# Expert weights loaded in 8 KB runs, projection steps of two k-tiles by 1024 columns, and moving tiles placed 32 bytes from the stationary ones

## The chip, the core and the metric

The kernel runs on one core of a Trainium2 chip. The metric is device time in microseconds of one execution. The matmul engine is TensorE (PE, with its weight loads as PEld), the elementwise engines are VectorE (DVE), ScalarE (ACT) and GpSimd (POOL); SyncE (SP) issues nearly all loads, in one queue.

## What is computed

Two transformer blocks of two layers each, on 256 tokens of width 1024, all in float32. Every layer starts from an adaptive projection of a condition vector to six vectors of 1024 (shift, scale and gate for two halves of the layer). The first block has two attentions and a feed-forward part with a short convolution; the second block has a mixer over tokens and a context, and 16 experts of which each takes the 32 tokens that score highest for it. In the first layer of the second block tokens and context go through the experts (two groups), in the last layer the tokens alone.

```python
mod = silu_c @ w_ada[l] + b_ada[l]                # 1024 -> 6 * 1024
sh1, sc1, gt1, sh2, sc2, gt2 = split(mod, 6)
h = modulate(rmsnorm(x, g_mix[l]), sh1, sc1)
x = x + gt1 * latent_mixer(h @ w_in[l], ...)
h2 = modulate(rmsnorm(x, g_ffn[l]), sh2, sc2)
...
def expert_choice_ffn(h, w_router, w_g, w_u, w_d):
    gate, idx = lax.top_k(softmax(h @ w_router), 32)     # tokens of each expert
    xs = h[idx]
    y = (silu(xs @ w_g) * (xs @ w_u)) @ w_d              # 1024 x 1024 each, 16 experts
    return zeros_like(h).at[idx].add(y * gate)
```

## The kernel before

Activations lie with channels on partitions, in eight k-tiles of 128 channels by 256 tokens. The dense matmuls work in split form: `split` (L226 to L228) writes a weight as a rounded high part `wh` (ACT, L227) and the rest `wl` (DVE, L228), activations likewise (`hh`, `hl`; in attention and feed-forward also in tiles `k1`, `k8`, `pt`), and `mm3` (L239 to L246) issues three products at L245: high by high, high by low, low by high. The stationary operand is the weight, the moving one the 256 tokens. In the trace's names buffer numbers are left out, so `k1`, `k8`, `k4` and `k2` all read `k`: into `dd`, `k` is a `k8` tile; into `acc`, a `k1` tile.

Tiles that matmuls read lie in pools, one behind the other (`PLACES`, L42): first the weights and their loads, then `hh`, `hl`, `k1`, `k8`, `pt`. Ahead of each pool stands a gap of `PADS` float32 words (L43). All tiles are multiples of 256 bytes, so the sum of the gaps so far gives a tile's place mod 256 against the weights (at 0): `hh` 64, `hl` 96, `k1` 128, `k8` 0, `pt` 32.

The adaptive projection is `ada` (L384 to L458). Part of its output, `DIRECT` (L37) blocks of 1024 columns, is made by `chunk`: one load of all eight k-tiles by 256 columns (in DRAM, runs of 1 KB), eight fp32 matmuls into four column tiles of one PSUM tile (L404), a DVE copy (L407), two PE transposes (L410), a reduction (L414) and the bias (L394). The other blocks are summed on DVE (L435 to L448) from loads of 4 KB runs. Eight chunks run at startup for the first layer, 24 for each layer of the second block as fillers between other work, from 476 to 1124 us; in the first block's second layer there are none.

The expert weights, three matrices of 1024 x 1024 for each of 16 experts, come as 192 loads of 1 MB a layer, in groups of four experts, issued by `expert_loads` (L1196 to L1231) through SP in the order of use; a load waits until its tile is free. A load holds two k-tiles, rows `(2 kp + k) P + p`, so that each of 128 partitions gets two runs of 4 KB. Loads with the tags `k4` and `whl` go to two tiles (`HALVES`, L40), each with a load of its own. In the last group the third matrix comes in columns of 256 instead, with runs of 1 KB. `product` (L1237) issues the fp32 matmuls at L1249: for each pair of k-tiles, each group of tokens, two k-tiles, two halves of 512 columns and four experts that share the array as column tiles. Its result is transposed at L1274 (eight transposes for each group of tokens and of experts), multiplied with the third matrix, and scattered back (L1282, L1283). The tokens are gathered ahead of it (L1161 to L1182) by a matmul with a one-hot matrix, whose stationary operand is 128 channels of the tokens (L1176 to L1180). The order of the instructions on PE between these parts is written by the tile planner when the program is built.

Of the kernel before, what the change touches and what calls it, by code (L numbers as in the profile page):

```python
# [13 lines left out]
OP = mybir.AluOpType  # L14
AX = mybir.AxisListType
PSUM = bass.MemoryType.PSUM

P = 128
S = 256
D = 1024  # L20
KT = D // P
# [4 lines left out]
N_EXP = 16  # L26
CAP = 32
GE = 4
# [11 lines left out]
HALVES = {"k4": ("k4", "k4"), "whl": ("wh", "wl")}  # L40
BUFS = {"k4": N4, "wh": NH, "wl": 3}
PLACES = [("wh", "wl", "w", "k2", "k4", "rx", "rr"), ("hh",), ("hl",), ("k1",), ("k8",), ("pt",)]  # L42
PADS = [0, 16, 8, 8, 32, 8]  # L43
PAD = 32

CONST_WIDTHS = [
# [79 lines left out]
class Kernel:  # L126
# [256 lines left out]

    def ada(self, w, cc, cs, bias, ns, direct):  # L384
        mod = self.t([P, ns, 48], "mod", 2)
        state = {}

        def bias_add(ps, c0, nj):
            for s in range(ns):
                i = bias[0][:, c0:c0 + nj]  # L390
                o = mod[:, s, c0:c0 + nj]
                if len(ps[s].shape) == 3:
                    o, i = (a.rearrange("p (g j) -> p j g", j=4) for a in (o, i))
                self.nc.vector.tensor_tensor(o, ps[s], i, op=OP.add)  # L394

        def chunk(c):
            def go():
                nc = self.nc
                t = self.wload(w, 0, KT, 256 * c, 256, tag=self.ada_tags.pop(0) if self.ada_tags else self.ada_tag)
                ad = self.ad()[:, :256]  # L400
                for i in range(2):
                    for g in range(4):
                        k = 2 * g + i
                        nc.tensor.matmul(ad[32 * g:32 * g + 32], cs[:, k], t[:, k], start=i == 0, stop=i == 1,  # L404
                                         skip_group_check=True)
                r = self.k1([P, 256])
                nc.vector.tensor_copy(r, ad)  # L407
                ps = self.mm((P, 2, P))
                for j in range(2):
                    nc.tensor.transpose(ps[:, j], r[:, j * P:(j + 1) * P], self.c("ident"))  # L410
                q = self.tiny([P, ns, 2])
                m = 32 // ns
                for s in range(ns):
                    nc.vector.tensor_reduce(q[:, s], ps[:, :, m * s:P:32], axis=AX.X, op=OP.add)  # L414
                bias_add([q[:, s] for s in range(ns)], 2 * c, 2)
            return go

        def total(b):
# [28 lines left out]
                            nc.vector.scalar_tensor_tensor(a, t[:, j], f, a, op0=OP.mult, op1=OP.add)  # L447
            return go  # L448

        todo = [chunk(c) for c in ([0, 4, 1, 5, 2, 6, 3, 7] if ns == 1 else range(8))[:4 * direct]]  # L450
        todo += [chunk(c) for c in range(8, 4 * direct)]
        for b in range(direct, 6):
            todo += [summed(b, c) for c in range(4)]
            if ns == 2 or b == 5:
# [698 lines left out]
    def again(self, x, a, b, r, put):  # L1153
        for k in range(KT):
# [3 lines left out]
            put(k, h)  # L1158
            yield

    def gather(self, s, th, tl, xs):  # L1161
        nc = self.nc
        e = slice(32 * s, 32 * s + N_EXP)
        ps = self.mm((P, 2, N_EXP))
        for t in range(2):
            nc.tensor.transpose(ps[:, t], self.sa[e, t * P:(t + 1) * P], self.c("ident")[e, e])
        st = self.k1([P, 2, N_EXP])
        nc.vector.tensor_copy(st, ps)
        hot = [self.k2([P, N_EXP, CAP], F32R) for _ in range(2)]
        for t in range(2):  # L1170
            nc.vector.tensor_tensor(hot[t], self.c("iota")[:, None, :].to_broadcast([P, N_EXP, CAP]),
                                    st[:, t, :, None].to_broadcast([P, N_EXP, CAP]), op=OP.is_equal)
        yield
        for k in range(KT):
            ps = self.mm()
            a = slice(k * P, (k + 1) * P)  # L1176
            for t in range(2):
                b = hot[t].rearrange("p e c -> p (e c)")
                nc.tensor.matmul(ps, th[:, t, a], b, start=t == 0, stop=False)
                nc.tensor.matmul(ps, tl[:, t, a], b, start=False, stop=t == 1)  # L1180
            nc.scalar.copy(xs[k // 4][:, k % 4], ps)
            yield  # L1182
# [13 lines left out]
    def expert_loads(self, l, early, ring):  # L1196
        ws = [self.io[n][l] for n in ("w_e_gate_2", "w_e_up_2", "w_e_down_2")]
        todo = [(ws[which][GE * gi + e], kp, which == 2 and gi == N_EXP // GE - 1) for gi in range(N_EXP // GE)
                for which in range(3) for kp in range(4) for e in range(GE)]
# [2 lines left out]

        def load(t, w, kp, cols, k, n):
            if cols:
                src = w[P * k:P * (k + n), 256 * kp:256 * kp + 256]
            else:
                src = w[(2 * kp + k) * P:(2 * kp + k + n) * P]
            self.nc.sync.dma_start(t, src.rearrange("(k p) n -> p k n", p=P))  # L1208

        def more(n):  # L1210
            late = []
# [21 lines left out]
    def experts(self, l, groups, gather, done):  # L1233
        nc, io = self.nc, self.io
# [20 lines left out]
        for gi in range(N_EXP // GE):  # L1255
# [11 lines left out]
            for s in range(ns):  # L1267
                tt = self.wl([P, KT, P], F32)
                for n in range(2):
                    a = acts[s][:, 512 * n:512 * n + 512]  # L1270
                    nc.vector.tensor_tensor(a, a, pu[s][n], op=OP.mult)  # L1271
                    ps = self.dd((P, 4, P))
                    for i in range(4):
                        nc.tensor.transpose(ps[:, i], a[:, i * P:(i + 1) * P], self.c("ident"))  # L1274
                    nc.scalar.copy(tt[:, 4 * n:4 * n + 4], ps)
                actt.append(tt)
            down = lambda s, k, e: actt[s][:, k, 32 * e:32 * e + 32]
# [208 lines left out]
```

## Time and profile before

| | us |
|---|---|
| median of the runs shown | 2833.57 |
| lowest and highest of them | 2826.25, 2837.12 |
| the profiled execution | 2828.94 |
| its span | 2827.2 |
| PE busy | 2637.7 (93%) |
| DVE busy | 1406.4 (50%) |
| ACT busy | 1023.5 (36%) |
| DMA, mean rate | 263 GB/s of 742.61 MB |

The span covers the first to the last instruction of the profiled execution; the remaining 1.7 us lie around it. The page of the profile shows shares over the whole span; what holds in one stage is read from the slices and from tables by stretches. In a row of instructions the first name is the tile that is written, behind the arrow stand the tiles that are read.

### The profile page before, as it was taken

How to read it: one execution, taken by the hardware profiler on the slowest of the kernel's cores; microseconds unless marked ns; L12 is line 12 of the kernel's file. 1: busy time of each engine (PE TensorE's matmuls, PEld its weight loads, DVE VectorE, ACT ScalarE, POOL GpSimd, SP SyncE). 2: the span in 40 equal slices, each digit the busy share in tenths (PEclk: the TensorE clock that was granted, in tenths of full speed). 3: DMA queues.
4: the chain of work that ended last, by engine and by line, in shares of the span. 5: the costliest groups of instructions: out<-in, count | busy, mean ns of one | idle time of the engine just before them, and what ended most of it. 6: DMA issues, size and time to landing. Idle time of an engine off the chain costs nothing.

```text
span 2827.2 us, 45431 instructions
## 1 busy us (share of the span) xinstructions
PE 2637.7 (93%) x18816; PEld 1835.7 (65%) x18816; DVE 1406.4 (50%) x2791; ACT 1023.5 (36%) x1906; POOL 123.2 (4%) x139
## 2 busy tenths in 40 slices
PE   7998999999999999989999999999989998878876
PEld 5898998888998689856994333333556994212122
DVE  6989977766778755776552010010577562000001
ACT  3564555554555644445453100000455452000000
POOL 0100001000000000120011000000021001000000
PEclk9999999999999999989999999999999999999999
DMA  8788855586455478412655999999712775999999
GB/s 310 242 314 290 309 176 169 186 277 240 163 193 191 151 257 266 138 43 80 204 164 221 366 401 404 420 388 409 248 60 75 250 235 222 420 420 420 421 420 344
DMA packets 397692, 742.61 MB, mean 263 GB/s; under 512 B 16214, under 2 KB 270126, under 8 KB 397486
## 3 DMA queue, kind: packets, MB, share of 16 engines
q1 hardware_dynamic: 396398, 738.66, 71.5%
q8 instruction: 148, 2.42, 0.3%
q10 hardware_dynamic: 1088, 1.05, 0.1%
q14 instruction: 58, 0.48, 0.0%
HBM read 738.61 MB, written 1.05 MB: 262 GB/s over the span
## 4 chain that ended last, share of the span: by engine, by line
PE 39%; DMA 12%; DVE 3%; POOL 1%; SPq 1%; ACT 1%; issue 0%; DVEq 0%; POOLq 0%; ACTq 0%
PE dd L245 12%; PE acc L1249 12%; PE mm L1249 5%; DMA w<-in_w_e_up_dram 2%; DMA k<-in_w_e_down_dram 2%; PE acc L941 2%; DMA w<-in_w_e_down_dram 2%; DMA k<-in_w_e_gate_dram 2%; DMA k<-in_w_e_up_dram 2%; DMA w<-in_w_e_gate_dram 2%; PE mm L970 1%; PE mm L964 1%; PE acc L1301 1%; PE dd L1282 1%; POOL k L756 1%; SPq L1208 1%
## 5 line engine op out<-in xcount | busy, mean ns | idle before, releaser
L245 PE MATMUL dd<-hh,wh 128*128 128x256 f32 x2384 | 684.4, 288 | 17.6 <-ACT hh L269 13.9
L228 DVE TENSOR_TENSOR wl<-w,wh 128x1024 fp32r<-128x1024 f32 (+1 forms) x534 | 554.5, 1042 | 276.7 <-ACT wh L227 275.2
L245 PE MATMUL dd<-hh,wl 128*128 128x256 f32 x2384 | 677.9, 285 | 5.6 <-DVE wl L228 5.6
L245 PE MATMUL dd<-hl,wh 128*128 128x256 f32 x2384 | 678.9, 285 | 0.7 <-DVE hl L481 0.5
L227 ACT CAST wh<-w 128x1024 fp32r<-128x1024 f32 (+1 forms) x534 | 477.9, 900 | 554.4 <-PE dd L245 424.4
L245 PEld LDWEIGHTS dd<-hh,wh 128*128 128x128 f32 x2384 | 454.2, 191 | 42.9 <-ACT hh L269 15.6
L245 PEld LDWEIGHTS dd<-hh,wl 128*128 128x128 f32 x2384 | 451.7, 190 | 12.5 <-DVE wl L228 6.9
L245 PEld LDWEIGHTS dd<-hl,wh 128*128 128x128 f32 x2384 | 452.6, 190 | 10.2 <-issue 7.2
L1249 PE MATMUL acc<-w,pt 128*32 128x512 f32 x624 | 222.9, 597 | 31.7 <-DMA w<-in_w_e_up_dram 17.0
L1271 DVE TENSOR_TENSOR wh<-wh,acc 128x512 f32<-128x512 f32 x20 | 13.7, 687 | 451.2 <-PE acc L1249 451.2
L1249 PE MATMUL acc<-k,pt 128*32 128x512 f32 x692 | 224.9, 597 | 8.7 <-DMA k<-in_w_e_up_dram 5.1
L245 PE MATMUL dd<-k,wh 128*128 128x256 f32 x896 | 168.6, 287 | 0.8 <-DVE k L655 0.5
L756 POOL TENSOR_TENSOR k<-k,rope 32x256 f32<-32x256 f32 (+1 forms) x96 | 86.8, 904 | 1820.7 <-DVE k L900 1332.4
L1249 PE MATMUL acc<-w,k 128*32 128x512 f32 x480 | 160.3, 603 | 0.7 <-ACT pt L1149 0.7
L1249 PE MATMUL acc<-w,wl 128*32 128x512 f32 x396 | 139.8, 600 | 15.9 <-DMA w<-in_w_e_down_dram 15.9
L1249 PE MATMUL acc<-k,wl 128*32 128x512 f32 x432 | 146.6, 600 | 5.1 <-DMA k<-in_w_e_down_dram 5.1
L245 PEld LDWEIGHTS dd<-k,wh 128*128 128x128 f32 x896 | 140.7, 192 | 4.5 <-DVE k L655 1.4
L1249 PE MATMUL acc<-k,k 128*32 128x512 f32 x376 | 133.4, 605 | 0.0
L1249 PEld LDWEIGHTS acc<-w,pt 128*32 128x32 f32 x624 | 45.8, 109 | 133.7 <-issue 69.9
L245 PE MATMUL dd<-k,wl 128*128 128x256 f32 x448 | 127.5, 285 | 2.1 <-DVE wl L228 2.1
L1283 DVE SCALAR_TENSOR_TENSOR x_res<-dd,mod,x_res 128x256 f32<-128x256 f32 x64 | 28.9, 483 | 173.0 <-PE dd L1282 173.0
L941 PE MATMUL acc<-k,k 64*128 64x512 f32 (+1 forms) x192 | 94.5, 606 | 14.8 <-ACT k L269 9.5
(351 smaller groups left out, 4408.5 us busy)
## 6 DMA issues: line engine op xcount, KB each, us to landing
w<-in_w_in_dram SPq DMA_DIRECT2D x104, 1024.0 KB
w<-in_w_ada_dram SPq DMA_DIRECT2D x63, 1024.0 KB
w<-in_w_e_gate_dram SPq DMA_DIRECT2D x54, 1024.0 KB
w<-in_w_e_up_dram SPq DMA_DIRECT2D x54, 1024.0 KB
w<-in_w_e_down_dram SPq DMA_DIRECT2D x48, 1024.0 KB
w<-in_w_up_dram SPq DMA_DIRECT2D x44, 1024.0 KB
k<-in_w_e_gate_dram SPq DMA_DIRECT2D x43, 1024.0 KB
k<-in_w_e_down_dram SPq DMA_DIRECT2D x43, 1024.0 KB
```

Source lines behind the costliest of these rows:

```text
L227: self.nc.scalar.copy(h, src)
L228: self.nc.vector.tensor_tensor(l, src, h.bitcast(F32), op=OP.subtract)
L245: self.last_mm = self.nc.tensor.matmul(ps, a, b, start=first and i == 0, stop=last and i == len(ops) - 1, skip_group_check=group)
L756: nc.gpsimd.tensor_tensor(u[dst], q[src], sin[src], op=OP.mult)
L941: nc.tensor.matmul(ps[:, :n], q[a, mt, qb * P:(qb + 1) * P], kk[a, br, lo:512], start=True, stop=not mask, skip_group_check=True)
L964: nc.tensor.transpose(pp[:, i], e[:, i * P:(i + 1) * P], self.c("ident"))
L970: nc.tensor.matmul(po[64 * f:64 * f + 64], vv[:, kt, P * br + 64 * f:P * br + 64 * f + 64], pt[:, f, i], start=i == 0, stop=i == len(kts) ...
L1208: self.nc.sync.dma_start(t, src.rearrange("(k p) n -> p k n", p=P))
L1249: nc.tensor.matmul(accs[s][n][32 * e:32 * e + 32], lhs(s, 2 * kp + k, e), tiles[e][k][:, 512 * n:512 * n + 512], start=kp == 0 and k == 0, ...
L1282: nc.tensor.matmul(ps, y[:, k * P:(k + 1) * P], maps[s][:, gi], start=True, stop=True)
L1283: nc.vector.scalar_tensor_tensor(x[:, k], ps, gate[:, k:k + 1], x[:, k], op0=OP.mult, op1=OP.add)
L1301: nc.tensor.matmul(ps[32 * e:32 * e + 32], down(s, k, e), tiles[e][k], start=k == 0, stop=k == KT - 1, skip_group_check=True)
```

## The change

Three things change. `PADS` moves the gaps: the places mod 256 become `hh` 32, `hl` 32, `k1` 160, `k8` 32, `pt` 32. The direct part of the projection goes in steps of two k-tiles by 1024 columns (runs of 4 KB): eight matmuls a step as before, four steps to a block of 1024 columns. With one condition vector (at startup) the four steps add up in one PSUM tile; with two, DVE copies the first and adds the others into a tile `adr`. Copy (or the last addition), two transposes and the bias follow only the fourth step; the reduction is gone. The expert loads, except the last group's columns, take rows `2 p + k` instead: a tile of two k-tiles gets one run of 8 KB on each partition, a half one of 4 KB at every 8 KB. Which channels a k-tile holds changes with it, so the stationary operands of the gather and of the transposes (first three groups) take every second column (`paired`).

```diff
--- before.py
+++ after.py
@@ -40,7 +40,7 @@
 HALVES = {"k4": ("k4", "k4"), "whl": ("wh", "wl")}
 BUFS = {"k4": N4, "wh": NH, "wl": 3}
 PLACES = [("wh", "wl", "w", "k2", "k4", "rx", "rr"), ("hh",), ("hl",), ("k1",), ("k8",), ("pt",)]
-PADS = [0, 16, 8, 8, 32, 8]
+PADS = [0, 8, 0, 32, 32, 0]
 PAD = 32
 
 CONST_WIDTHS = [
@@ -383,36 +383,47 @@
 
     def ada(self, w, cc, cs, bias, ns, direct):
         mod = self.t([P, ns, 48], "mod", 2)
-        state = {}
+        state, hold = {}, ns == 1
 
         def bias_add(ps, c0, nj):
             for s in range(ns):
                 i = bias[0][:, c0:c0 + nj]
                 o = mod[:, s, c0:c0 + nj]
                 if len(ps[s].shape) == 3:
-                    o, i = (a.rearrange("p (g j) -> p j g", j=4) for a in (o, i))
+                    o, i = (a.rearrange("p (g j) -> p j g", j=ps[s].shape[1]) for a in (o, i))
                 self.nc.vector.tensor_tensor(o, ps[s], i, op=OP.add)
 
-        def chunk(c):
+        def direct_step(b, c):
             def go():
                 nc = self.nc
-                t = self.wload(w, 0, KT, 256 * c, 256, tag=self.ada_tags.pop(0) if self.ada_tags else self.ada_tag)
-                ad = self.ad()[:, :256]
-                for i in range(2):
+                t = self.wload(w, 2 * c, 2, 1024 * b, 1024, tag=self.ada_tags.pop(0) if self.ada_tags else self.ada_tag)
+                if hold:
+                    ad = state[b] = self.acc((P, 256)) if c == 0 else state[b]
+                else:
+                    ad = self.ad()[:, :256]
+                for j in range(2):
                     for g in range(4):
-                        k = 2 * g + i
-                        nc.tensor.matmul(ad[32 * g:32 * g + 32], cs[:, k], t[:, k], start=i == 0, stop=i == 1,
+                        nc.tensor.matmul(ad[32 * g:32 * g + 32], cs[:, 2 * c + j], t[:, j, 256 * g:256 * g + 256],
+                                         start=j == 0 and (c == 0 or not hold), stop=j == 1 and (c == 3 or not hold),
                                          skip_group_check=True)
-                r = self.k1([P, 256])
-                nc.vector.tensor_copy(r, ad)
+                if hold:
+                    if c < 3:
+                        return
+                    r = self.k1([P, 256])
+                    nc.vector.tensor_copy(r, ad)
+                elif c == 0:
+                    r = state[b] = self.t([P, 256], "adr", 1)
+                    nc.vector.tensor_copy(r, ad)
+                else:
+                    r = state[b]
+                    nc.vector.tensor_tensor(r, r, ad, op=OP.add)
+                if c < 3:
+                    return
                 ps = self.mm((P, 2, P))
                 for j in range(2):
                     nc.tensor.transpose(ps[:, j], r[:, j * P:(j + 1) * P], self.c("ident"))
-                q = self.tiny([P, ns, 2])
                 m = 32 // ns
-                for s in range(ns):
-                    nc.vector.tensor_reduce(q[:, s], ps[:, :, m * s:P:32], axis=AX.X, op=OP.add)
-                bias_add([q[:, s] for s in range(ns)], 2 * c, 2)
+                bias_add([ps[:, :, m * s:P:32] for s in range(ns)], 8 * b, 8)
             return go
 
         def total(b):
@@ -447,8 +458,7 @@
                             nc.vector.scalar_tensor_tensor(a, t[:, j], f, a, op0=OP.mult, op1=OP.add)
             return go
 
-        todo = [chunk(c) for c in ([0, 4, 1, 5, 2, 6, 3, 7] if ns == 1 else range(8))[:4 * direct]]
-        todo += [chunk(c) for c in range(8, 4 * direct)]
+        todo = [direct_step(b, c) for b in range(direct) for c in range(4)]
         for b in range(direct, 6):
             todo += [summed(b, c) for c in range(4)]
             if ns == 2 or b == 5:
@@ -1158,6 +1168,9 @@
             put(k, h)
             yield
 
+    def paired(self, k):
+        return slice(256 * (k // 2) + k % 2, 256 * (k // 2) + 256, 2)
+
     def gather(self, s, th, tl, xs):
         nc = self.nc
         e = slice(32 * s, 32 * s + N_EXP)
@@ -1173,7 +1186,7 @@
         yield
         for k in range(KT):
             ps = self.mm()
-            a = slice(k * P, (k + 1) * P)
+            a = self.paired(k)
             for t in range(2):
                 b = hot[t].rearrange("p e c -> p (e c)")
                 nc.tensor.matmul(ps, th[:, t, a], b, start=t == 0, stop=False)
@@ -1202,10 +1215,10 @@
 
         def load(t, w, kp, cols, k, n):
             if cols:
-                src = w[P * k:P * (k + n), 256 * kp:256 * kp + 256]
+                src = w[P * k:P * (k + n), 256 * kp:256 * kp + 256].rearrange("(k p) n -> p k n", p=P)
             else:
-                src = w[(2 * kp + k) * P:(2 * kp + k + n) * P]
-            self.nc.sync.dma_start(t, src.rearrange("(k p) n -> p k n", p=P))
+                src = w[2 * kp * P:(2 * kp + 2) * P].rearrange("(p k) n -> p k n", k=2)[:, k:k + n]
+            self.nc.sync.dma_start(t, src)
 
         def more(n):
             late = []
@@ -1271,7 +1284,8 @@
                     nc.vector.tensor_tensor(a, a, pu[s][n], op=OP.mult)
                     ps = self.dd((P, 4, P))
                     for i in range(4):
-                        nc.tensor.transpose(ps[:, i], a[:, i * P:(i + 1) * P], self.c("ident"))
+                        b = slice(i * P, (i + 1) * P) if gi == N_EXP // GE - 1 else self.paired(i)
+                        nc.tensor.transpose(ps[:, i], a[:, b], self.c("ident"))
                     nc.scalar.copy(tt[:, 4 * n:4 * n + 4], ps)
                 actt.append(tt)
             down = lambda s, k, e: actt[s][:, k, 32 * e:32 * e + 32]
```

## Rows read from the trace of the kernel before

**Rows 1.** Page, span in 40 slices: PE's busy tenths, and the transfer rate.
```profile
PE   7998999999999999989999999999989998878876
...
GB/s 310 242 314 290 309 176 169 186 277 240 163 193 191 151 257 266 138 43 80 204 164 221 366 401 404 420 388 409 248 60 75 250 235 222 420 420 420 421 420 344
```

**Rows 2.** Table by stretches: busy us (count) PE, PEld, DVE, ACT, POOL; clock, DMA, GB/s.
```profile
11.00:28.00 17.00, 13.71 (x119) 8.00 (x123) 9.31 (x30) 5.47 (x13) 0.00 (x0) 1.00 1.09 385
100.00:350.00 250.00, 239.87 (x1884) 227.37 (x1884) 234.48 (x362) 135.90 (x225) 0.00 (x0) 0.99 0.86 303
1560.00:1960.00 400.00, 399.02 (x2652) 138.33 (x2646) 33.51 (x68) 24.91 (x45) 0.00 (x0) 0.99 0.99 398
2400.00:2750.00 350.00, 282.22 (x1210) 74.91 (x1203) 15.84 (x32) 11.36 (x20) 0.00 (x0) 1.00 1.03 420
```

**Rows 3.** Waits of the SP queue, 1560 to 1960 us: us in total, times, longest.
```profile
SPq L1208 <- PE mm L1249: 224.3, 31, 15.3
```

**Rows 4.** Page, costliest groups: split matmuls by moving tile, busy us, mean ns.
```profile
L245 PE MATMUL dd<-hh,wh 128*128 128x256 f32 x2384 | 684.4, 288 | 17.6 <-ACT hh L269 13.9
...
L245 PE MATMUL dd<-k,wh 128*128 128x256 f32 x896 | 168.6, 287 | 0.8 <-DVE k L655 0.5
```

**Rows 5.** Instructions of L245: matmuls into acc, ns min/median/max, first and last start.
```profile
L245 PE MATMUL acc<-k,wh x528: 274/281/388, 269.7 to 877.3; 128*128 128x256 f32 x176
```

**Rows 6.** Timeline of PE: start, us, line, operation, tiles, shape, count.
```profile
189.30 0.28 PE L245 MATMUL dd<-k,wl 128*128 128x256 f32 x1
...
202.74 0.36 PE L245 MATMUL dd<-k,wl 128*128 128x256 f32 x1
...
1329.49 0.28 PE L245 MATMUL dd<-hh,wh 128*128 128x256 f32 x1
...
1359.55 0.28 PE L245 MATMUL dd<-hh,wl 128*128 128x256 f32 x1
...
2342.34 0.28 PE L245 MATMUL dd<-pt,wl 128*128 128x256 f32 x1
...
2343.74 0.28 PE L245 MATMUL dd<-pt,wl 128*128 128x256 f32 x1
```

**Rows 7.** Table by stretches, PE alone: busy (count), granted clock, DMA share, GB/s.
```profile
189.25:202.68 13.43, 13.43 (x114) 1.00 1.01 368
1329.45:1359.50 30.05, 30.05 (x255) 1.00 0.78 276
2342.30:2343.70 1.40, 1.40 (x14) 1.00 1.04 383
```

**Rows 8.** Timeline of PE around one pair of projection transposes.
```profile
600.05 0.38 PE L410 MATMUL mm<-cst,k 128*128 128x128 f32 x2
...
600.18 0.36 PE L245 MATMUL dd<-hh,wl 128*128 128x256 f32 x1
```

**Rows 9.** Instructions of L410: count, ns min/median/max, first and last start.
```profile
L410 PE MATMUL mm<-cst,k x112: 270/272/330, 19.1 to 1123.7; 128*128 128x128 f32 x112
```

**Rows 10.** Timeline of PE at startup: one projection chunk and its transposes.
```profile
17.50 1.07 PE L404 MATMUL ad<-w,k 128*32 128x256 f32 x16 [0.32 <-DVE c L336]
...
19.11 0.44 PE L410 MATMUL mm<-cst,k 128*128 128x128 f32 x2 [0.55 <-DVE k L407]
```

**Rows 11.** Chain that ended last, experts with two groups: start us, us, what.
```profile
1739.02 2.65 PE acc L1249 x19
...
1748.59 2.65 PE acc L1249 x19
...
1762.44 7.24 PE dd L1282 x32
...
1781.87 2.65 PE acc L1249 x19
...
1792.29 2.65 PE acc L1249 x19
```

**Rows 12.** Instructions of L1274: weight loads of the experts' transposes.
```profile
L1274 PEld LDWEIGHTS dd<-cst,wh x96: 138/141/230, 1596.1 to 2778.7; 128*128 128x128 f32 x96
```

## What the change will do to the time

> **What bounds the kernel now.** I read the forty slices first [rows 1]: PE is busy nine tenths or more of nearly every slice up to slice 34, and only from there on does it drop to seven or eight tenths while the transfer rate stands still at 420 GB/s. So there are two kernels in one: nearly everything up to 2365 us is bound by the PE, the last layer's experts by the DMA queue. The table by stretches says the same with numbers [rows 2]: from 100 to 350 us PE is busy 239.87 of 250 us, from 1560 to 1960 us 399.02 of 400, from 2400 to 2750 us 282.22 of 350 with the DMA engines at 1.03 of their share. The stretch from 1560 to 1960 us (experts of the layer with two groups) has both near their limit, 398 GB/s beside a full PE; the waits of the SP queue settle which one rules: it waited 224.3 us there for matmuls of L1249 to give tiles free [rows 3], so PE rules and the loads follow. The first 35 us are a third case: DMA share 1.09 at 385 GB/s [rows 2], and PE in short bursts between round trips.
>
> **The sum is made against the profiled execution**, 2828.94 us (span 2827.2). The median of the runs shown is 2833.57, which is 4.6 us above it; I carry the differences over to the median.
>
> **Part 1, startup.** Eight projection loads of 1 MB stand in the saturated queue. In runs of 1 KB the queue gives 385 GB/s, in runs of 4 KB 420 (both in [rows 2]): 1.0486 MB cost 2.724 and 2.497 us. Eight loads save 8 x 0.227 = 1.8 us. The PE steps go from a cycle of about 2 us (17.50 to the transposes at 19.11 and on, [rows 10]) to some 1.1 us for three steps of four, since copy, transposes, reduction and bias come only with every fourth; the eight steps can end before the last load now, and the loads set the end. I take 1.8; up to 5 if the relieved DVE also brings the first weight splits forward.
>
> **Part 2, cadence of the split matmuls.** A 128x256 matmul on split operands starts every so many ns, and that differs with the moving tile. Steps counted between two starts [rows 6, 7]: k8 (same place as its stationary) 189.30 to 202.74, 112 steps (114 in the stretch, two of which began before): 120.0 ns. hh and hl (64 and 96 bytes away, mod 256): 1329.49 to 1359.55, 254 steps (one of 255 began before): 118.3 ns. pt (32 bytes away): 2342.34 to 2343.74, 12 steps: 116.7 ns. The granted clock is 1.00 in all three, and the DMA share is 1.01, 0.78 and 1.04, so neither clock nor transfers order them. The change puts hh, hl, k8 and pt at 32 and k1 at 160. I take 117.0 after it, because 12 steps read to 0.01 us leave a step open by nearly 1 ns. Counts: hh,wh, hl,wh and hh,wl 2384 each, so 7152 x 1.3 = 9.3 us; k,wh 896 and half as many k,wl, 1344 x 3.0 = 4.0 us [rows 4]; acc from k1 528 and half as many with wl, 792 [rows 5], for which I take half of hh's step, 0.65, so 0.5 us. Together 13.8. It isn't all on the path: between 100 and 350 us the DVE is busy 234.48 us beside PE's 239.87 [rows 2], so of the 2.8 us there (1884 matmuls at most, by 1.5) I count half, and a tenth of the rest for waits on splits: 11 us. Ends: 0, and with 116.7 for all, 7152 x 1.6 + 1344 x 3.3 + 792 x 3.3 = 18.5.
> One thing speaks against this term: hl was already at 32 mod 64, and the steps of hh and hl together give one even 118.3. So mod 64 alone isn't the rule; I rest on the distance that pt has, 32 mod 256.
> The Trainium skill speaks against the whole term: by SBUF — State Buffer, section SBUF: two separate sides, PE never waits on anyone at its port, and by TensorE: Matmul & The Clock Gate (the step that loads the stationary operand) the two operands come through independent read ports, so placement should change nothing. The trace differs, 116.7 against 120.0 for equal shapes; but those are different tiles at different places of the program, so only a run can settle it. It is rival A.
>
> **Part 3, transposes of the projection.** 56 chunks make 112 transposes now [rows 9]; after it 14 pairs remain, and of the 42 pairs removed 36 lie in the PE-bound part (the 24 direct steps of each of the second block's layers). A pair delays the next matmul by 0.13 to 0.14 us (600.05 to 600.18, [rows 8]): 36 x 0.135 = 4.9 us. The eight matmuls of a step stay. On DVE a copy becomes an addition of the same size and reductions and narrow bias additions go; DVE isn't the bound there, so I count nothing.
>
> **Part 4, expert loads where DMA is the bound.** From [rows 2], 1 KB and 4 KB runs differ by 0.227 us per load for 768 runs, 0.296 ns a run. A load in 8 KB runs has 128 fewer: 0.038 us. Of the last layer's 192 loads 17 are asked for ahead, 16 are column loads with 1 KB runs as before, and some 20 are halves, whose runs stay 4 KB: 139 x 0.038 = 5.3 us. No row shows 8 KB runs on this queue. Ends: nothing, and all that runs still cost, 256 x 0.296 = 0.076 us a load, 10.5 us.
> DMA: Bandwidth & Descriptors, section Why small descriptors are slow, in the Trainium skill agrees that each packet has a fixed cost, and gives a ceiling of the path of 435 GB/s; by that ceiling the term would be at most 139 x (2.497 - 2.41) = 12 us, an estimate from that page. The trace's 420 GB/s lies well above the 358 that the page calls the limit of HBM, so that limit doesn't hold here.
>
> **Part 5, expert loads where PE is the bound.** From 1560 to 1960 us faster loads are hidden [rows 2, 3]: 0. But the order of the matmuls is written when the program is built, by what the planner expects of loads, and one pair of k-tiles takes 9.57 us in one place (1739.02 to 1748.59) and 10.42 in another (1781.87 to 1792.29), with 64 matmuls each [rows 11]. Any shift in the planner's times can move this. I take 0, ends -15 and +37 (rivals B and C).
>
> **Part 6, strided stationary operands.** Rows 2p+k in a tile make the transposes and the gather read every second column as stationary. 72 of 96 transposes of L1274 are touched, whose weight load takes 141 ns [rows 12]; the gather's are hidden behind 512-column matmuls. If each load doubled and nothing hid it, 54 of them in the PE-bound layer cost 7.6 us; I take 0.5.
>
> **Sum:** -1.8 - 11 - 4.9 - 5.3 + 0 + 0.5 = -22.5 us; 2828.94 becomes 2806, the median 2833.57 becomes 2811.
>
> **Rivals.** *A, placement does nothing.* For it: the even 118.3 of hh and hl. Against: pt's 116.7 under full DMA load. Then -11.5 and 2822, within half a per cent.
> *B, the two-group expert stage gets shorter.* Its PE time of a group, 12 passes of 9.57 to 10.42 and 7.24 us of scattering [rows 11], about 124 us, stands above the loads' 48 x 2.46 = 118; if the order tightens, each of three groups can fall by 5 to that floor: -15 more, 2796. For it: the loads are the planner's input. Against: SP's waits say that the order, not the loads, is late now.
> *C, slower: the same stage is written with the long pass throughout.* 44 passes (four groups, three products, four pairs, without the last group's down) at 0.85 us more each are 37 us, 2811 + 37 = 2848. It eats up the whole gain from 27 passes on and is slower by over half a per cent from 43. Both lengths stand in the trace, so it isn't far-fetched; nothing in the change lengthens the matmuls themselves.
> *D, 8 KB runs move no faster than 4 KB* (they are cut up on the way): 2816. Not told from the forecast by time alone.
> *E, C in part, or strided loads in full:* 2822 to 2840.
>
> **How the numbers follow.** Forecast with D: 0.48 (2799 to 2819). B 0.18 (2785 to 2799). A 0.19. E 0.10. C 0.05. A measurement of this kernel can tell about half a per cent, 14 us, from no change: faster by more than that means under 2819.4, forecast and B, 0.66; within it A and E, 0.29; slower C, 0.05. The range leaves out C and the lower half of B, and E's worst: 2792 to 2832.
>
> **What would show it.** Starts of the hh and hl matmuls every 117 ns instead of 118.3, of k8's every 117 instead of 120.0; if they stand where they were, A. A rate of about 427 GB/s from 2400 to 2750 us instead of 420; if 420, D. 28 transposes of the projection instead of 112. The first split matmul 1.8 us earlier. Pass lengths in the two-group stage: 9.57 mostly means the forecast, under 9.5 B, 10.4 throughout C. Weight loads of the transposes at 141 ns as now, or longer for part 6. The prediction is wrong, above all, if the written order of the two-group stage moves by more than the other parts together.

## The result and the profile after

| | before, us | after, us |
|---|---|---|
| median | 2832.85 | 2801.0 |
| profiled execution | 2828.94 | 2800.99 |
| its span | 2827.2 | 2799.2 |
| PE busy | 2637.7 | 2615.0 |
| DVE busy | 1406.4 | 1385.1 |

The ratio is 0.9891 (95% interval 0.9879 to 0.9903): 31.9 us less, where 22.5 were forecast. (The kernel before has one run more here than in the table ahead of the prediction, so its median is 2832.85 and not 2833.57.) The time lies inside the range; of the shares behind it one is wrong by a factor of three, and the runs below can't tell the others from what was forecast.

The page of the kernel after, packets and transfer rate in 40 slices (answering [rows 1]):

```profile
GB/s 313 239 316 286 322 177 154 208 286 260 176 187 181 147 288 258 122 46 113 184 174 239 366 406 400 425 379 407 243 49 83 251 239 235 424 425 424 424 425 330
DMA packets 315002, 742.59 MB, mean 265 GB/s; under 512 B 16214, under 2 KB 212782, under 8 KB 275118
```

Some 40,000 packets of 8 KB and more are there now (315002 less 275118), so the runs are not cut up, and the last slices stand at 424 and 425 where they stood at 420. The table by stretches, same columns as [rows 2], for the expert stage with two groups and for the last layer:

```profile
1535.80:1936.40 400.60, 399.62 (x2648) 140.40 (x2642) 33.51 (x68) 24.96 (x45) 0.00 (x0) 0.99 0.97 398
2373.90:2720.50 346.60, 282.78 (x1207) 75.74 (x1202) 15.86 (x32) 11.37 (x20) 0.00 (x0) 1.00 1.01 424
```

The same work of the last layer takes 346.60 instead of 350 us; the stage with two groups is as full of PE as before, and between the same instructions near 1560 and 1960 us of the kernel before it is 0.9 us longer. The timeline of PE, two starts each of hh/hl and of k8 matmuls (answering [rows 6]):

```profile
180.07 0.28 PE L245 MATMUL dd<-hh,wh 128*128 128x256 f32 x1
...
185.20 0.28 PE L245 MATMUL dd<-hh,wl 128*128 128x256 f32 x1
...
611.03 0.28 PE L245 MATMUL dd<-k,wl 128*128 128x256 f32 x1
...
618.03 0.28 PE L245 MATMUL dd<-k,wl 128*128 128x256 f32 x1
```

44 steps in 5.13 us and 60 in 7.00: 116.6 and 116.7 ns, where 118.3 and 120.0 stood [rows 6]. And the projection's transposes, by instruction (answering [rows 9]):

```profile
L424 PE MATMUL mm<-cst,adr x24: 270/272/329, 513.6 to 1100.7; 128*128 128x128 f32 x24
...
L424 PE MATMUL mm<-cst,k x4: 272/300/328, 20.5 to 32.7; 128*128 128x128 f32 x4
```

28 of 112, as forecast. Setting equal instructions of the two traces side by side gives where the time went: 0.5 us by the first split matmul, 0.6 by 476 us, 23.0 by 1124 us, 24.5 by 1515, 23.6 by 2005, 25.7 by 2365 and 28 by the end. Most of it lies between 476 and 1124 us, the stretch where the second block's projection runs between other work, and to which the prediction gave 4.9 us and a part of the spacing.

### The profile page after: what moved, and what is told of

It is laid out like the page before. It is cut to its first block, busy times and chain, and to the rows that moved or that the text cites. A ratio compares the mean times of both kernels' runs of the same rounds, so it can differ in the third digit from the quotient of the medians.

```text
span 2799.2 us, 45103 instructions
## 1 busy us (share of the span) xinstructions
PE 2615.0 (93%) x18732; PEld 1818.9 (65%) x18732; DVE 1385.1 (49%) x2603; ACT 1023.7 (37%) x1906; POOL 123.2 (4%) x139
## 2 busy tenths in 40 slices
DMA packets 315002, 742.59 MB, mean 265 GB/s; under 512 B 16214, under 2 KB 212782, under 8 KB 275118
## 4 chain that ended last, share of the span: by engine, by line
PE 39%; DMA 14%; DVE 3%; POOL 1%; ACT 1%; SPq 1%; issue 0%; DVEq 0%; POOLq 0%; ACTq 0%
PE dd L245 12%; PE acc L1262 11%; PE mm L1262 5%; DMA k<-in_w_e_down_dram 3%; DMA w<-in_w_e_up_dram 2%; DMA k<-in_w_e_up_dram 2%; DMA w<-in_w_e_down_dram 2%; DMA k<-in_w_e_gate_dram 2%; PE acc L951 2%; DMA w<-in_w_e_gate_dram 2%; PE mm L980 1%; PE mm L974 1%; PE acc L1315 1%; PE dd L1296 1%; POOL k L766 1%; PE mm L1192 1%
## 5 line engine op out<-in xcount | busy, mean ns | idle before, releaser
L245 PE MATMUL dd<-hh,wh 128*128 128x256 f32 x2384 | 683.9, 288 | 14.3 <-ACT hh L269 12.8
L245 PE MATMUL dd<-hh,wl 128*128 128x256 f32 x2384 | 675.5, 284 | 5.0 <-DVE wl L228 4.9
L245 PE MATMUL dd<-hl,wh 128*128 128x256 f32 x2384 | 675.6, 284 | 0.5 <-DVE hl L491 0.3
L245 PEld LDWEIGHTS dd<-hh,wh 128*128 128x128 f32 x2384 | 453.7, 191 | 39.2 <-ACT hh L269 14.5
L245 PEld LDWEIGHTS dd<-hh,wl 128*128 128x128 f32 x2384 | 454.0, 191 | 12.6 <-DVE wl L228 6.3
L245 PEld LDWEIGHTS dd<-hl,wh 128*128 128x128 f32 x2384 | 455.0, 191 | 7.9 <-issue 5.3
L1262 PE MATMUL acc<-w,pt 128*32 128x512 f32 x624 | 222.9, 597 | 31.2 <-DMA w<-in_w_e_up_dram 16.2
L1284 DVE TENSOR_TENSOR wh<-wh,acc 128x512 f32<-128x512 f32 x20 | 13.8, 688 | 450.0 <-PE acc L1262 450.0
L245 PE MATMUL dd<-k,wh 128*128 128x256 f32 x896 | 164.7, 284 | 0.8 <-DVE k L665 0.8
L245 PEld LDWEIGHTS dd<-k,wh 128*128 128x128 f32 x896 | 138.0, 189 | 4.5 <-DVE k L665 1.7
L245 PE MATMUL dd<-k,wl 128*128 128x256 f32 x448 | 125.7, 281 | 2.1 <-DVE wl L228 2.1
L1262 PEld LDWEIGHTS acc<-k,pt 128*32 128x32 f32 x692 | 46.3, 109 | 95.0 <-issue 63.9
```

Source lines behind the costliest of these rows:

```text
L245: self.last_mm = self.nc.tensor.matmul(ps, a, b, start=first and i == 0, stop=last and i == len(ops) - 1, skip_group_check=group)
L1262: nc.tensor.matmul(accs[s][n][32 * e:32 * e + 32], lhs(s, 2 * kp + k, e), tiles[e][k][:, 512 * n:512 * n + 512], start=kp == 0 and k == 0, ...
```

## The experiments

| kernel | median us | ratio to before | 95% interval |
|---|---|---|---|
| places_only | 2826.36 | 0.9973 | 0.9955 to 0.999 |
| steps_only | 2814.32 | 0.9926 | 0.9907 to 0.9945 |
| loads_only | 2828.0 | 0.998 | 0.9967 to 0.9992 |
| all_at_32 | 2802.0 | 0.9881 | 0.9862 to 0.99 |
| steps_startup | 2830.13 | 0.9985 | 0.9972 to 0.9998 |
| steps_fillers | 2817.3 | 0.9946 | 0.9928 to 0.9963 |
| quarter | 2819.54 | 0.9951 | 0.9932 to 0.9971 |
| startup_busy | 2830.47 | 0.9988 | 0.9977 to 0.9999 |
| all_at_0 | 2844.23 | 1.0044 | 1.003 to 1.0057 |
| relief | 2829.15 | 0.9988 | 0.9972 to 1.0003 |
| relief_places | 2823.91 | 0.9977 | 0.9963 to 0.9992 |
| wide_last | 2803.6 | 0.9896 | 0.9878 to 0.9914 |

The kernel before stood at 2833.66 us beside the first four, 2833.46 beside the next four, 2832.52 beside the last four. So each kernel is compared with runs of the kernel before from its own round. The intervals given behind a difference below are those of the ratio, in us. The three parts alone give 7.3, 19.3 and 5.7 us, together 32.3: within their intervals they add up to the whole.

### The places alone

```diff
-PADS = [0, 16, 8, 8, 32, 8]
+PADS = [0, 8, 0, 32, 32, 0]
```

> The kernel before with the gaps of the change alone. Theory: the spacing of the split matmuls is set by the place of the moving tile; hh, hl and k8 start every 116.7 to 117.8 ns as in the changed kernel (118.3 and 120.0 before), but between 37 and 476 us, where DVE is nearly as busy as PE, this is given back as waits, so the gain comes from 476 to 1515 and 2005 to 2365 us alone: 8 to 10 us of the 31, ratio near 0.997. Rival of the prediction as it stood: 11 us with part of it before 476 us. Rival A: spacings as in the kernel before, no gain.

Measured: 7.3 us less (2.8 to 12.8). Placement does something: rival A falls. The ten runs stand in two groups, five from 2817.57 to 2822.65 and five from 2830.08 to 2832.89, so the median lies in a gap and says little about the size. Next, all gaps at zero in the kernel before:

```diff
-PADS = [0, 16, 8, 8, 32, 8]
+PADS = [0, 0, 0, 0, 0, 0]
```

> The kernel before with all gaps at zero: every moving tile starts at the same place mod 256 as the stationary ones. If the place sets the spacing, hh, hl, k1, k8 and pt all start every 119.7 to 120.0 ns as k8 did before, and the kernel is 3 to 6 us slower (5700 or so split matmuls outside the first layer by 1.5 ns, less what waits take up). If the 120.0 of k8 belonged to its stretches of the program and not to its place, the spacings stay at 118.3 for hh and hl, 116.7 for pt, and so does the time.

Measured: 11.7 us more (8.5 to 16.1), twice to four times what was expected. Set side by side with the kernel before, its trace is 7.9 us behind at the first split matmul, which belongs to the startup (below), and loses another 12.5 us from there to the end, with PE's order almost unchanged. The timeline of PE in this kernel, hh and hl in a stretch of the program where they started every 118.3 ns before:

```profile
1349.01 0.28 PE L245 MATMUL dd<-hh,wl 128*128 128x256 f32 x1
...
1354.29 0.28 PE L245 MATMUL dd<-hl,wh 128*128 128x256 f32 x1
```

44 steps in 5.28 us: 120.0 ns, what k8 had in [rows 6]. The same tiles, the same work, moved by 64 and 96 bytes. So the 120.0 of k8 was its place: with the distance mod 256 to the stationary tile, the spacing of hh, hl, k8 and pt is 120.0 at 0, 116.7 at 32 and 118.3 at 64 and 96. From all at 0 to the change's places it is 19.0 us, 11.7 more and 7.3 less than the kernel before. 3.3 ns on 7152 matmuls of hh and hl, 1344 of k8 and, for pt, which moves too, 624 would be 30 us; some 0.6 of it arrive at the end.

All moving tiles at 32, in the changed kernel:

```diff
-PADS = [0, 8, 0, 32, 32, 0]
+PADS = [0, 8, 0, 0, 0, 0]
```

> The changed kernel with k1 at 32 too (gaps 0, 8, 0, 0, 0, 0 words: every moving tile 32 bytes from the stationary ones, mod 256). If the place mod 256 sets the spacing, k1's matmuls go from 117.5 to 119.9 ns to 116.7 and the time falls by 1 to 2 us. If only the place mod 64 counts, k1 at 160 and at 32 are the same and nothing changes.

Measured: 2802.0 beside 2801.0 of the changed kernel; no difference that these runs can tell, where 1 to 2 us less were expected. What k1 at 32 is worth stays below a few us. Its spacing does change. k1 into acc, in the changed kernel:

```profile
820.61 0.40 PE L245 MATMUL acc<-k,wh 128*128 128x256 f32 x2
...
822.65 0.28 PE L245 MATMUL acc<-k,wl 128*128 128x256 f32 x1
```

in places_only:

```profile
839.52 0.40 PE L245 MATMUL acc<-k,wh 128*128 128x256 f32 x2
...
841.51 0.28 PE L245 MATMUL acc<-k,wl 128*128 128x256 f32 x1
```

and in all_at_32:

```profile
818.47 0.40 PE L245 MATMUL acc<-k,wh 128*128 128x256 f32 x2
...
820.46 0.28 PE L245 MATMUL acc<-k,wl 128*128 128x256 f32 x1
```

Each is 17 steps: 2.04 us or 120.0 ns with k1 at 160 in the changed kernel, 1.99 us or 117 ns with k1 at 160 in places_only, 117 ns at 32. Of the 45 stretches of seven and more such matmuls in the changed kernel 23 step at 120 ns and 10 at 117; in places_only 32 of 45 step at 117. So 160, which is 32 mod 64, is not the same as 32, and the place mod 64 is not the rule. But one place mod 256 also gives two spacings for k1, so the place mod 256 is not the whole rule either; what else counts was not tested.

Where the rest of the spacing's gain goes: beside the one trace of the kernel before, that of places_only wins only 1.1 us between the first split matmul and 476 us. Two kernels test whether DVE is what takes it there.

```diff
-                for j in range(2):
+                for j in range(1 if ns == 1 else 2):
                     for s, a in enumerate(state[b]):
```

> The kernel before with half of the DVE work of the first block's summed projection left out (every second of the two k-tiles, L447), a cut of some 51 us of DVE time before 500 us. It is the base for the next kernel. If DVE paces the first layer, 37 to 476 us gets several us shorter; if PE does, nothing moves.

The same with the gaps of the change:

> The same with the gaps of the change. Theory: with DVE relieved PE paces the first layer, and the closer spacing (1.6 ns for hh and hl, 3 for k8, some 2100 and 240 matmuls) now shortens 37 to 476 us by 3 to 4 us against the kernel with the relief alone, where the gaps alone gave 0.4 us. Rival: the gain before 476 us is lost to something else than DVE, and stays below 1 us.

Measured: the relief alone changes the time by 3.4 us with an interval that takes in zero, and from the first to the 2501st split matmul (37 to some 412 us) 375.6 us become 373.9. The busy times of that stretch, before and with the relief:

```profile
37.00:476.00 439.00, 417.12 (x3228) 394.24 (x3228) 385.03 (x604) 239.62 (x404) 12.16 (x9) 0.98 0.72 252
```

```profile
37.00:476.00 439.00, 419.80 (x3236) 396.93 (x3240) 344.12 (x564) 239.16 (x405) 10.89 (x9) 0.97 0.72 252
```

DVE falls from 385.03 to 344.12 us (the third busy time) and PE stays. With the relief the gaps shorten the same 2500 steps from 373.9 to 370.7 us, by 3.2; without it from 375.6 to 374.7, by 0.9. That looks like the theory, but the other traces on record take it back. The seven kernels with the old gaps and all of the DVE's work (before, loads_only, the three with new steps, quarter, startup_busy) need 375.6 to 377.6 us for these steps, the middle one 376.9; the four with hh, hl and k8 at 32 (places_only, the changed kernel, all_at_32, wide_last) need 374.3 to 374.7. So the gaps win some 2.5 us here without the relief too, and the trace of the kernel before is the shortest of its kind. Of the 3.2 us with the relief up to 1.6 belong to the granted clock: its shares missing to 1.00 add up to 11.3 us in one trace and 9.7 in the other. DVE as the taker is not shown; where the rest of the gain goes stays open.

### The projection steps alone

```diff
-        def chunk(c):
+        def direct_step(b, c):
...
-        todo = [chunk(c) for c in ([0, 4, 1, 5, 2, 6, 3, 7] if ns == 1 else range(8))[:4 * direct]]
-        todo += [chunk(c) for c in range(8, 4 * direct)]
+        todo = [direct_step(b, c) for b in range(direct) for c in range(4)]
```

> The kernel before with the new projection steps alone. The prediction's price: 4.9 us for 36 pairs of transposes and 1.8 us at startup, 6.7 us. Theory after reading the changed kernel: startup gives only 0.5 us, but a pair of transposes that goes also takes a break of the split stream with it (waits of about 0.1 us behind it), so 476 to 1124 us gets 10 to 14 us shorter: 10 to 14 us in all, ratio near 0.996. If the extra gain came from the places instead, 6 us.

Measured: 19.3 us less (15.6 to 26.4), three fifths of the whole, and above both prices expected. The same part cut in two, new steps at startup alone and in the second block alone:

```diff
...
+        if ns == 1:
+            todo = [direct_step(b, c) for b in range(direct) for c in range(4)]
+        else:
+            todo = [chunk(c) for c in ([0, 4, 1, 5, 2, 6, 3, 7] if ns == 1 else range(8))[:4 * direct]]
+            todo += [chunk(c) for c in range(8, 4 * direct)]
```

> The kernel before with the new steps for the first layer's projection alone (startup); the second block keeps its chunks. Theory: with full clock at startup this gives next to nothing (0.5 us in the changed kernel's trace), but in some runs the granted clock stays at 0.50 through the chunks, each cycle takes 3.1 instead of 2.0 us, and the first split matmul comes 6 to 7 us later; the new steps wait for loads at either clock. So the spread of the kernel before (some 13 us) shrinks to about 4 and the median falls by 3 to 5 us. Rival of the prediction: 1.8 us in every run, spread as before.

```diff
...
+        if ns == 2:
+            todo = [direct_step(b, c) for b in range(direct) for c in range(4)]
+        else:
+            todo = [chunk(c) for c in ([0, 4, 1, 5, 2, 6, 3, 7] if ns == 1 else range(8))[:4 * direct]]
+            todo += [chunk(c) for c in range(8, 4 * direct)]
```

> The kernel before with the new steps for the second block alone. Theory: 14 to 17 us less (the profile of both step parts together lost 18 us between 476 and 1124 us and won 1 to 3 elsewhere), and the spread of the kernel before stays. Rival of the prediction: 4.9 us.

Measured: 3.3 us at startup (0.6 to 7.9), 16.2 in the second block (10.5 to 20.4). Is it the runs of the loads or the copies and transposes that pay there? The kernel before, with 1 KB runs, and three of four chunks ending after their matmuls:

```diff
+                if ns == 2 and c % 4 < 3:
+                    for s in range(ns):
+                        nc.vector.tensor_copy(mod[:, s, 2 * c:2 * c + 2], bias[0][:, 2 * c:2 * c + 2])
+                    return
                 r = self.k1([P, 256])
```

> The kernel before, loads in 1 KB runs and chunks as they are, but of the second block's chunks only every fourth is copied, transposed, reduced and biased; for the other three the projection is left out and the bias alone is written, in two small DVE copies. If the removed transposes with their copies are what pays, this gives what the new steps in the second block give, 12 to 17 us. If it is the 4 KB runs of the loads, it gives 5 to 7 us (36 pairs at 0.135 to 0.2 us).

Measured: 13.9 us less (8.2 to 19.3), with the 1 KB runs in place. So the copies, transposes and reductions together make most of it; a share of the runs of a few us is not excluded. Why 14 to 16 us and not 4.9? Three things, read from the traces.

First, the pair itself. The timeline of the kernel before, one row further than [rows 8]:

```profile
600.05 0.38 PE L410 MATMUL mm<-cst,k 128*128 128x128 f32 x2
600.18 0.36 PE L245 MATMUL dd<-hh,wl 128*128 128x256 f32 x1
600.39 0.28 PE L245 MATMUL dd<-hh,wh 128*128 128x256 f32 x1
```

The first matmul behind the pair lasts 0.36 us instead of 0.28, and the one behind it starts 0.21 after it instead of 0.12. From 600.05 to 600.39 it is 0.34 us for a pair and a matmul that alone takes 0.12: a pair costs 0.22 us, not 0.135. 36 pairs are 7.9 us. Of the pairs in the kernel before 35 stand so between split matmuls, and all but one look like this: 0.14 us ahead of the next matmul, 0.08 behind it.

Second, the clock. Between the first block and the second the granted clock fell before, by stretches of 4 us (PE alone: busy, count, granted clock, DMA share, GB/s):

```profile
668.00:672.00 4.00, 2.75 (x14) 0.84 1.09 386
672.00:676.00 4.00, 3.62 (x13) 0.73 1.09 386
...
680.00:684.00 4.00, 3.69 (x20) 0.62 1.07 372
684.00:688.00 4.00, 4.00 (x34) 0.95 0.35 121
```

and the same work in steps_fillers:

```profile
672.00:676.00 4.00, 2.43 (x17) 1.00 1.03 417
676.00:680.00 4.00, 3.20 (x15) 1.00 1.01 373
680.00:684.00 4.00, 3.36 (x39) 1.00 0.62 189
```

PE was partly idle in both before that point: busy 2.75 and 2.43 of 4 us. The shares missing to 1.00 (0.16, 0.27, 0.38, 0.05) make 3.4 us. A fall between 660 and 700 us is in the traces of all eight kernels with all chunks in the second block (3.4 us in five of them, 1.7 in three), and in none of the six with the steps or with a quarter of the copies. What keeps the clock up was not told apart.

Third, waits. From 476 to 1124 us in the kernel before and over the same work in steps_only:

```profile
476.00:1124.00 648.00, 637.62 (x5260) 567.68 (x5259) 445.26 (x1016) 334.04 (x629) 9.13 (x9) 0.99 0.64 215
```

```profile
478.70:1108.70 630.00, 622.67 (x5187) 557.41 (x5187) 429.39 (x849) 333.55 (x629) 9.13 (x9) 1.00 0.65 221
```

PE idles 10.4 us of the first and 7.3 of the second: 3.1 us. This is the least certain of the three: in steps_fillers, with the same steps in this stretch, PE idles 9.3 us. The three make 14.4 us. The trace of steps_only shows 18.0 for this stretch, so 3.6 us of it have no name here; that of steps_fillers shows 15.5.

At startup it is another story. The first split matmul of the kernel before, in its profiled execution, whose granted clock was 1.00 from 11 to 28 us [rows 2]:

```profile
37.21 0.58 PE L245 MATMUL dd<-hh,wh 128*128 128x256 f32 x1 [2.21 <-ACT wh L227]
```

In that of places_only, whose startup is that of the kernel before but for the gaps:

```profile
18.92 1.93 PE L404 MATMUL ad<-w,k 128*32 128x256 f32 x16
...
22.02 1.93 PE L404 MATMUL ad<-w,k 128*32 128x256 f32 x16
...
44.33 0.58 PE L245 MATMUL dd<-hh,wh 128*128 128x256 f32 x1 [2.46 <-ACT wh L227]
```

```profile
28.00:40.00 12.00, 9.81 (x73) 3.24 (x71) 3.01 (x12) 0.00 (x0) 0.00 (x0) 0.50 1.06 348
```

The granted clock is 0.50, the lower of the two levels, the matmuls of a chunk take 1.93 instead of 1.07 us [rows 10], a chunk 3.1 instead of 2.0, and the first split matmul comes at 44.33. Eight traces on record have these startup chunks. In five (before, loads_only, quarter, relief, relief_places) the first split matmul comes at 36.7 to 38.0 us, in three (places_only, steps_fillers, all_at_0) at 43.0 to 45.1, and in these three the granted clock reads 0.50 from some 20 us or earlier until past 50. So the startup has two lengths, some 7 us apart, and the profiled execution of the kernel before had the short one. That fits its place 4.6 us below the median: all five early executions lie below the median of their kernel, all three late ones 5 to 7 us above. The timeline of PE in steps_startup, also at half clock:

```profile
27.38 1.94 PE L428 MATMUL acc<-k,k 128*32 128x256 f32 x16 [0.52 <-DMA k<-in_w_ada_dram]
...
36.65 0.58 PE L245 MATMUL dd<-hh,wh 128*128 128x256 f32 x1 [2.47 <-ACT wh L227]
```

Its steps wait for loads, and at half clock the first split matmul still comes at 36.65 us. The spread of its runs is 10.6 us (2824.1 to 2834.73), where the theory said 4. A matmul of no use, set into PE's wait for the copy in each startup chunk of the kernel before, tests the clock from the other side:

```diff
+                if ns == 1:
+                    spare = self.acc((P, 256))
+                    nc.tensor.matmul(spare, self.c("ident"), t[:, 0], start=True, stop=True)
                 r = self.k1([P, 256])
```

> The kernel before with one matmul more in each startup chunk, into a spare PSUM tile that nobody reads, placed where PE waits for the DVE copy. Theory: the granted clock is 1.00 through the chunks in all runs, the late starts are gone, the spread shrinks to some 4 us at 2828 to 2831. If the late starts come from the loads or elsewhere, spread and median stay at 2829 to 2841 and 2834.

Measured: 3.0 us less (0.3 to 6.5), though it adds work; the timeline of PE:

```profile
18.86 1.07 PE L404 MATMUL ad<-w,k 128*32 128x256 f32 x16
19.86 0.70 PE L408 MATMUL acc<-w,cst 128*128 128x256 f32 x2
...
37.09 0.38 PE L245 MATMUL dd<-hh,wh 128*128 128x256 f32 x1 [1.81 <-ACT wh L227]
```

The granted clock was 1.00 through the chunks in this execution. The times spread over 8 us (2825.74 to 2834.15), where the kernel before spread over 14 (in 21 runs, not 10) and the theory said 4. So the startup clock fits as a cause of the spread and is not the only one; the profiled execution of startup_busy started early and was still 5 us behind the kernel before by 650 us.

### The expert loads alone

```diff
...
-                src = w[(2 * kp + k) * P:(2 * kp + k + n) * P]
-            self.nc.sync.dma_start(t, src.rearrange("(k p) n -> p k n", p=P))
+                src = w[2 * kp * P:(2 * kp + 2) * P].rearrange("(p k) n -> p k n", k=2)[:, k:k + n]
+            self.nc.sync.dma_start(t, src)
```

> The kernel before with the expert loads in 8 KB runs, and with the strided stationary operands that belong to them. Prediction: 5.3 us less in the last layer, 0.5 us more elsewhere, 4.8 us in all. Theory after reading the changed kernel: 424 instead of 420 GB/s from 2400 to 2750 us gives 3 to 4 us, the tail gives 1 us back, the experts with two groups cost 0.9 us more: 1.5 to 3 us less in all. If 8 KB runs moved no faster, 0.9 us more than before.

Measured: 5.7 us less between medians (2.3 to 9.3), above the 1.5 to 3 of the theory and near the 4.8 of the prediction; 3.6 between the profiled executions, of which the last layer gives 5.4 and the stretch up to 2365 us costs 1.8. The rate of the last layer is 426 GB/s in its trace (424 in the changed kernel's) instead of 420. Rival D falls. The strided stationary operands of the changed kernel, by instruction (answering [rows 12]):

```profile
L1288 PEld LDWEIGHTS dd<-cst,wh x96: 137/209/226, 1571.8 to 2749.2; 128*128 128x128 f32 x96
```

The median goes from 141 to 209 ns. The 226 belong to a stretch at granted clock 0.50 (1576 to 1582 us); the 230 that [rows 12] show as the longest for neighbouring columns belong to one too (1600 to 1605). The 64 transposes of the layer with two groups take 0.5 us more on PE for it, start to start. For the gather no cost shows: its 64 matmuls there take 17.9 us before, 18.5 in the changed kernel and 18.1 in loads_only, but also 18.3 in wide_last, where their stationary operands are contiguous. Can the 0.5 us be saved, by 8 KB runs in the last layer alone?

```diff
...
+        if not self.wide:
+            return slice(k * P, (k + 1) * P)
...
-                src = w[2 * kp * P:(2 * kp + 2) * P].rearrange("(p k) n -> p k n", k=2)[:, k:k + n]
+                src = w[2 * kp * P:(2 * kp + 2) * P].rearrange("(p k) n -> p k n" if self.wide else "(k p) n -> p k n", k=2)[:, k:k + n]
...
-            last = l == n2 - 1
+            last = self.wide = l == n2 - 1
```

> The changed kernel with all moving tiles at 32, and the 8 KB runs in the last layer alone; the experts with two groups load in 4 KB runs, with contiguous stationary operands, as in the kernel before. Theory: those loads are hidden there and the strided weight loads cost 0.9 us, so 1 us less than the changed kernel: 2799 to 2801.

Measured: 2803.6 us, ratio 0.9896 where the changed kernel has 0.9891 and all_at_32 0.9881; the 2799 to 2801 expected did not come. A difference of 1 us can't be told by these runs, and none of the variants is faster than the changed kernel by more than they can tell.

## Why the prediction was right and where it was not

**Part 1, startup: over-sized in the trace, and silent on the clock.** I priced 1.8 us of loads; the first split matmul comes 0.5 us earlier in the profiled executions. Between medians it is 3.3 us (0.6 to 7.9), which takes in 1.8. The late starts at half clock, 7 us, would explain a larger gain between medians; the profiled execution before did not show them, since its 15 to 33 us stood at full clock. The gap of 4.6 us between it and the median was on the page, and I carried it over as a constant where it seems to have a cause.

**Part 2, cadence: mechanism right, size not refuted.** 116.6 to 116.7 ns came as the rows of pt said, and hl's even spacing was no counter-evidence: k1 at 160 shows that 32 mod 64 is not the rule. The half step forecast for k1 did not come in the changed kernel, where about half of its stretches step at 120 ns. For the share on the path I took 0.8, that is 11 us; measured are 7.3 us, about half of the 13.8 worked out, but the interval of 2.8 to 12.8 takes in the 11. As I read the section of the Trainium skill that I cited for rival A (SBUF — State Buffer, section SBUF: two separate sides), all_at_0 should have equalled the kernel before; measured is 11.7 us more, so for these matmuls the measurement decides against that reading.

**Part 3, transposes: the step that failed.** Forecast 4.9, measured 16.2 us (10.5 to 20.4) for the second block. The term "a pair delays the next matmul by 0.13 to 0.14" stopped at the next start, where the row's own duration of 0.36 said that the one after it is late too: 0.22. "I count nothing" for DVE and the waits left out 1.0 to 3.1 us by the two traces with the new steps there, and the granted clock of the stretch, which I didn't read by slices, another 1.7 to 3.4. With the 7.9 us of pairs that is most of what was measured; what keeps the clock up, and the rest, stay open.

**Parts 4 and 6, loads in the last layer and strided operands:** forecast 4.8 together, measured 5.7 (2.3 to 9.3); 424 instead of 427 GB/s. The 0.5 us for the strided operands is what the transposes cost; that each load gets half as long again I had only within a bound. That bound counts 54 strided transposes in the layer with two groups; the trace has 48 (three of four groups with 16 each), which makes it 6.8 us and not 7.6.

**Part 5, the stage with two groups:** the two pairs of k-tiles that took 9.57 and 10.42 us take the same in the changed kernel, and the stage is 0.9 us longer, of which the transposes above are 0.5; rivals B and C did not occur.

The total came out inside the range although part 3 missed by 11 us. That is in part luck: the range was wide because of rivals that did not occur, and part 2 came out 4 us lower, the other way. By the time alone the measured 2801 lies nearer to rival B's 2796 than to the forecast's 2811; only the unchanged length of the two-group stage tells them apart.

## What to carry to other kernels

A small interruption of a dense matmul stream is to be priced from the last undisturbed start before it to the first regular step behind it, and the granted clock is to be read around each place where PE idles, before the change and after: between 660 and 700 us it fell here in every kernel with all the interruptions and in none without most of them. A profiled execution that lies several us from the median may have a cause that a second profile can show, and one trace beside one other is a weak base for a few us: with seven traces the gain in the first 2500 steps was 2.5 us where one had said 0.9. Equal matmuls at different spacings are worth a look at where their operands lie: 32 bytes from the stationary tile instead of 0 was worth 2.8% of each here, instead of 64 and 96 1.4%.

## What the hardware showed that was not expected

The spacing of 128x256 split matmuls goes from 120.0 to 116.7 ns with the moving tile's place against the stationary one; for k1 the same place mod 256 showed 117 and 120. The first matmul behind two fp32 transposes lasts 0.36 us instead of 0.28. A weight load of 128x128 fp32 with every second column takes 209 ns in the middle (193 to 219) instead of 141 at full clock; at half clock it takes 226 and one of neighbouring columns 230. At startup the granted clock stood at 0.50 in three executions and at 1.00 in five of nearly the same work, worth 7 us there.
